# A four-layer trunk on one core: input combinations traced in five pieces, MLP loads held back, other buffers for the gating layer's first weights

## The chip, the core and the metric

The kernel runs on one core of a Trainium2 chip. The engines it uses are TensorE (PE: matmuls, and PEld for the weight loads that overlap them), VectorE (DVE), ScalarE (ACT), GpSimd (POOL: a few small operations and the DMAs that add into their target) and SyncE (SP: the plain loads). The metric is the device time of one execution in microseconds, as the median of several.

## What is computed

A trunk of two token mixers, each followed by a dense MLP, for one sequence of 512 tokens and a width of 1024, all in float32:

```python
def sq_relu_mlp(h, w_up, w_down):
    return jnp.square(jax.nn.relu(h @ w_up)) @ w_down

def chunked_sgu_mixer(h, w_in, ln_g, ln_b, w_spatial, b_spatial, w_out):
    z = jax.nn.gelu(h @ w_in, approximate=False)
    u, v = jnp.split(z, 2, axis=-1)
    v = layer_norm(v, ln_g, ln_b)
    # 128x128 lower triangular mixing of positions, one matrix per channel group
    v = ...
    return (u * v) @ w_out

# layer 0: latent attention, MLP; layer 1: spatial gating, MLP; every one is
# x = x + f(rms_norm(x)); a last rms_norm at the end
```

The gating layer's `w_in` is 1024 x 4096 and its `w_out` 2048 x 1024; each MLP's `w_up` is 1024 x 4096 and `w_down` 4096 x 1024.

## The kernel before

The stages run one after the other: attention until about 170 us of the trace, the first MLP until about 503, the gating layer until about 770, the second MLP until 1098. PE does the products of the last three as sums of three fp32r products: each operand is split into a high part, a cast on ACT (`split`, L125; `wh` for a weight, `g` or `q` for an activation), and a low part, a subtraction on DVE (`low`, L122; `wl` for a weight), and high x high, high x low and low x high are added in PSUM (L110).

On top of this, the large products use a scheme of seven block products instead of eight for 2 x 2 blocks. The blocks of the normed input are A11, A12, A21, A22, and the seven left operands are A11, A12, A22, S3 = A11 - A21, N1 = A22 - A21, S2 = -N1 - A11 and S4 = -A12 - S2. `Quarters` makes them: `first` makes A11 and S3, `rest` transposes the second half of the input (`turn`: PE transposes, then ACT scales one half of each of four banks into A12 and DVE the other into A22) and makes the five others. Each of the seven is split in a high and a low part. The weights' combinations come from DMAs: a block is loaded by SP (`load`, L991), and others are added into the same buffer by POOL's accumulating DMA (`add`, L994) once the buffer's earlier content has been split.

An *item* is one block product: `prepare` fetches and splits its weights, `go` issues its matmuls (48 of 256 columns in an MLP, 24 of 512 columns in the gating layer) and what uses its sum. Items are traced in a list; each is prepared two items ahead. The program of every engine is then ordered by a scheduler that follows the traced order and its own estimate of when data is there, so code that is traced at another place moves instructions on ACT and DVE. All loads on SP stand in one queue and all accumulations on POOL in another; each waits for its target buffer to be free.

In an MLP (`ffn`, `up`) the first items are m1 (A11, weights b), m5 (S3, weights a), m2 (A12, weights c), m6 (S2, weights a + b), m7 (N1, weights p3: b with a block added), m3 (A22, weights p4: a with a block added), m4 (S4). They are called items 0 to 6 below. Items 0, 3, 4 and 6 add into the same two PSUM banks X; between items 3 and 4 ACT copies both banks out (`keep`, L1073), and item 4 adds on. The raw weights are in six buffers (`raws`), two of them shared with the stage before. All of `rest` was traced right behind item 0.

The gating layer begins with `gate(0)` and `gate(1)`, whose items alternate: A11 of both (items 0 and 1), A12 of both (items 2 and 3), N1 of both, S4 of both, and so on. Items 2 and 3 use weights c and c1. Before, both were loaded into one buffer, W, so the load of c1 waited for the split of c. The other raw buffers are R1, R2, and U1 and U2, the halves of `u0`; `rest` wrote A12, A22 and N1 into `u0` too, so U1 and U2 came free only behind it.

Of the kernel before, what the change touches and what calls it, by code (L numbers as in the profile page):

```python
# [10 lines left out]
F32 = mybir.dt.float32  # L11
# [6 lines left out]
P = 128  # L18
T = 512
# [38 lines left out]
def trunk(ctx: ExitStack, tc: tile.TileContext, a):  # L58
# [10 lines left out]
    def nm(s):  # L69
        count[0] += 1  # L70
        return f"{s}_{count[0]}"
# [21 lines left out]
    def tmp(shape=(P, T), tag="t", **kw):  # L93
        return scratch[-1].tile(list(shape), F32, tag=tag, name=nm(tag), **kw)
# [19 lines left out]
    def gpair(t=None):  # L114
# [3 lines left out]
        t = t.rearrange("p k n -> p (k n)")  # L118
        return t[:, 0:T], t[:, T : 2 * T]

    def low(eng, l, src, h):
        return eng.tensor_sub(l, src, h.bitcast(F32))  # L122

    def split(hl, src, eng=None):
        nc.scalar.copy(hl[0], src)  # L125
        low(eng or nc.vector, hl[1], src, hl[0])
        return hl
# [103 lines left out]
    def diagonals(r):  # L231
        dg = tmp((P, NT, P))
        nc.vector.tensor_tensor(
            out=dg, in0=ident.unsqueeze(1).broadcast_to([P, NT, P]),
            in1=r.unsqueeze(2).broadcast_to([P, NT, P]), op=ALU.mult,
        )
        return dg.rearrange("p i q -> p (i q)")

    def row_form(dg, parts=False):

        ps = psum()
        if not parts:
            nc.tensor.matmul(ps, lhsT=ones, rhs=dg, start=True, stop=True)
        else:
            h, l = dg
            nc.tensor.matmul(ps, lhsT=ones_r, rhs=h, start=True, stop=False)
            nc.tensor.matmul(ps, lhsT=ones_r, rhs=l, start=False, stop=True)
        rb = tmp(tag="rb", bufs=1)
        nc.scalar.copy(rb, ps)
        return rb  # L250

# [38 lines left out]
    def four(dtype=F32R):  # L290
        return gxp.tile([P, 4, H], dtype, tag="g", name=nm("g"))
# [7 lines left out]
    class Quarters:  # L299
# [28 lines left out]

        def rest(self, a12, a22, n1):

            self.turn(1, a12, a22)
            stt = nc.vector.scalar_tensor_tensor
            nc.vector.tensor_sub(n1, a22, self.a21)
            s2, s4 = self.a11, a12
            stt(out=s2, in0=n1, scalar=-1.0, in1=self.a11, op0=ALU.mult, op1=ALU.subtract)
            self.A12 = split((four(), G6[0]), a12)
            stt(out=s4, in0=a12, scalar=-1.0, in1=s2, op0=ALU.mult, op1=ALU.subtract)
            self.S2 = split((G6[1], G6[2]), s2)
            self.N1 = split((G6[3], G6[4]), n1)
            self.A22 = split((G6[5], four()), a22)  # L340
            self.S4 = split((four(), four()), s4)

# [215 lines left out]
    with tc.tile_pool(name="att", bufs=1) as att:  # L560
# [356 lines left out]
        def go(n):  # L917
            for _ in range(min(n, len(waiting))):
                waiting.pop(0)()
# [76 lines left out]
    def ffn(layer, xq, norm, pool, after=None, last=None, mid=None):  # L996
# [24 lines left out]
        def up(c):  # L1021
# [116 lines left out]
            m3 = item(p4, "A22", "Y", False, end3, True)  # L1138
            m4 = item(w22, "S4", "X", False, end4, True)
            if c == 0:  # L1140
                begin = m1[1]

                def first():
                    begin()
                    three = [squares.get() for _ in range(3)]
                    xq.rest(*three)
                    for t in three:
                        squares.put(t)
                    nc.vector.reciprocal(r2, norm.mean())
                    nc.vector.tensor_scalar(  # L1150
                        out=nr2, in0=r2, scalar1=-1.0, scalar2=None, op0=ALU.mult
                    )

                return [(m1[0], first), m5, m2, m6, m7, m3, m4], sq
            return [m1, m2, m5, m6, m7, m3, m4], sq

        def accumulate(i, u, ps, r):
# [131 lines left out]
        n_mixed = len(work)  # L1289
        if last is None:  # L1290
            work += down(3, sq)
        ahead = 2
        for prepare, _ in work[:ahead]:
            prepare()
        for j, (_, go) in enumerate(work):
            if j == 1:
                spare[:] = banks[6:8]
            if j == 7:
                spare[:] = []
            if j == n_mixed:  # L1300
                spare[:] = banks[0:2]
            go()
            if j + ahead < len(work):
                work[j + ahead][0]()
        if last is not None:
            spare[:] = banks
            last(
# [23 lines left out]
    gx2 = Quarters("norm_ffn", KD, 1)  # L1331
    with stage(1), tc.tile_pool(name="sgu", bufs=1) as sg:
        w_in, w_out = a["sgu_w_in"][0], a["sgu_w_out"][0]
        wt = sg.tile([P, 8, P], F32, name="wt")
        Bt = sg.tile([P, 16, P], F32, name="Bt")


        v = [sg.tile([P, NT, 1024], F32, name=nm("v")) for _ in range(2)]
        stats = sg.tile([P, P], F32, name="stats")
        st = stats[:, 0:96].rearrange("p (i c e) -> p i c e", i=NT, c=4)  # L1340
        mv = stats[:, 96:104].rearrange("p (i e) -> p i e", e=2)

        names = ("a11", "a12", "a21", "a22")
        u0 = sg.tile([P, NT, 1024], F32, name="u0")
        uq = [
            {t: o[:, n, :].rearrange("p (k n) -> p k n", k=4) for n, t in enumerate(names)}
            for o in (u0, v[0])
# [7 lines left out]


        R1, R2 = (raw_tile((P, 4, 512)) for _ in range(2))
        W = sg.tile([P, 4, 512], F32, name=nm("wb"))
        U1, U2 = halves_of(u0)
        V1, V2 = halves_of(v[1])  # L1360
        BT = Bt.rearrange("p (k a) t -> p k (a t)", k=4)
# [105 lines left out]
        def gate(c, X, Y, slots):  # L1467
            sa, sb, sc = slots
            na, nb = f"a{c}", f"b{c}"

            def w(k, u):
                return wview(w_in, gx1.row(k), 512, SGW + c * 1024 + u * 512, 512)

            def at(name, b):

                t, u = int(name[1]) - 1, int(name[2]) - 1
                i = 2 * t + b
                return i, v[c][:, i, u * 512 : (u + 1) * 512], st[:, i, 2 * c + u, :]

            def keep(name, acc):  # L1480
                for b in range(2):
                    nc.scalar.copy(at(name, b)[1], acc[b])

            def plus(name, acc):
                for b in range(2):
                    t = at(name, b)[1]
                    nc.vector.tensor_add(t, t, acc[b])

            def gelu(name, r, acc=None):
                for b in range(2):  # L1490
                    i, t, sums = at(name, b)
                    nc.scalar.activation(
                        t, t if acc is None else acc[b], AF.Gelu, scale=norms[r][:, i : i + 1]
                    )
                    nc.vector.bn_stats(out=sums, in_=t)

            def end1():
                keep("a11", X)

            def end2():  # L1500
                plus("a11", Y)
                gelu("a11", "r")

            def end5():
                keep("a22", Y)

            def end3():
                keep("a12", Y)

            def end6():  # L1510
                plus("a12", X)
                gelu("a12", "nr")

            def end7():
                plus("a22", X)
                gelu("a22", "nr")

            def end4():
                gelu("a21", "r", X)

            def p2():
                nc.vector.tensor_add(s[na], s[na], s[nb])

            def item(acc, first, left, *args):
                return rows_item(acc, first, lambda: getattr(gx1, left), *args)

            return [
                item(X, True, "A11", na, lambda: get(na, sa, w(0, 0)), end1),
                item(Y, True, "A12", "c", lambda: get("c", sc, w(1, 0)), end2),
                item(Y, True, "N1", na, lambda: add(sa, w(0, 1)), end5),  # L1530
                item(Y, False, "S4", nb, lambda: get(nb, sb, w(1, 1)), end3, p2),
                item(X, False, "S2", na, lambda: None, end6),
                item(X, False, "S3", nb, lambda: add(sb, w(0, 1)), end7),
                item(X, False, "A22", na, lambda: add(sa, w(1, 0)), end4),
            ]
# [101 lines left out]
        def outer(X, Y, Z):  # L1637
# [64 lines left out]
            return items  # L1702

        work = [
            i for two in zip(gate(0, A, E, (R1, U1, W)), gate(1, B, C, (R2, U2, W))) for i in two
        ]
        work += other(0, A, E, C, (R1, W, R2, W)) + other(1, C, E, A, (R2, R1, W, R1))
        work += outer(A, C, E)
# [2 lines left out]
        def after(n, f):  # L1711
            then.setdefault(n, []).append(f)

        def begin():
            gx1.rest(*(uq[0][t] for t in ("a11", "a12", "a21")))
            r = inv_sqrt(norm1.mean())
            with tc.issue_after(root[0].ins):
                mix_load()
            norms["r"], norms["nr"] = r, small()
            nc.vector.tensor_scalar(  # L1720
                out=norms["nr"], in0=r, scalar1=-1.0, scalar2=None, op0=ALU.mult
            )

        def rows_of_r():
            norms["rb"] = row_form(diagonals(norms["r"]))

        def deviations():
            for i in range(NT):
# [20 lines left out]
            spare[:] = t  # L1749

        after(0, begin)
        after(6, lambda: banks_are(E))
        after(8, rows_of_r)
        after(9, lambda: (mix_transposed(0), mix_transposed(1)))
# [20 lines left out]
        ahead = 2  # L1775
        for prepare, _ in work[:ahead]:
            prepare()
        for j, (_, go) in enumerate(work):
            go()
            for f in then.get(j, ()):  # L1780
                f()
            if j + ahead < len(work):
                work[j + ahead][0]()
        fixed[0] = None


# [115 lines left out]
```

## Time and profile before

| | |
|---|---|
| median of 3 runs | 1096.78 us (1094.18 to 1101.85) |
| the profiled execution | 1099.8 us, of which its span is 1098.1 us |
| busy share of the span | PE 97%, PEld 87%, DVE 79%, ACT 57%, POOL 12% |
| mean granted clock of PE | 0.984 of full speed |
| moved by DMA | 163.33 MB, 149 GB/s in the mean |
| share of the chain that ended last | PE 84%, DVE 7%, DMA 3%, ACT 3% |

The profile is of one execution. A row of the timeline gives the start and the busy time of an instruction or a run of like ones, and in brackets how long its engine stood still before it and which instruction released it. The windows give each engine's busy time in a stretch and PE's granted clock there. PE is the engine that is hardly ever idle, so its few idle times and its stretches at a lower clock are what to look for; idle time of ACT or DVE matters only where PE waits for what they do next.

### The profile page before, as it was taken

Reading aid. Unit: us, or ns where it says so; the run is one execution under the profiler, and the core shown is the slowest. Engines: PE = TensorE matmul, PEld = TensorE weight load, DVE = VectorE, ACT = ScalarE, POOL = GpSimd, SP = SyncE. Lnnn points to the kernel's source line nnn. Section 1 sums busy time; section 2 is a strip of 40 time slices with the busy share of each in tenths; the row PEclk is TensorE's granted clock in tenths of the full one; section 3 lists DMA queues with packets and bytes.
Section 4 is the critical chain, followed back from the end, with each engine's and each line's share of the span. In section 5 each row is a group of like instructions: output and inputs, shape, how many; then the busy total and the mean of one; then the engine's idle time right before and its main releaser. Section 6 shows DMA issues by size and latency. Waiting matters only on the chain.

```text
span 1098.1 us, 15748 instructions
## 1 busy us (share of the span) xinstructions
PE 1062.3 (97%) x6540; PEld 950.8 (87%) x6540; DVE 865.7 (79%) x947; ACT 628.7 (57%) x714; POOL 128.3 (12%) x155
## 2 busy tenths in 40 slices
PE   8799999999999999999899999999999999999997
PEld 6688888999998999877788999888899999999986
DVE  6988756897887887886868588997988788888753
ACT  4577646665655655646655635556775555556541
POOL 5510000001001001003011000110001001001000
PEclk9999999899999999989899999999999999999999
DMA  6120147668668759348386836876785876756431
GB/s 203 39 78 16 63 115 220 181 147 176 197 153 192 178 135 224 116 77 192 116 158 140 236 71 201 230 121 166 173 228 120 221 196 115 224 125 117 116 113 58
DMA packets 86083, 163.33 MB, mean 149 GB/s; under 512 B 4917, under 2 KB 10620, under 8 KB 85884
## 3 DMA queue, kind: packets, MB, share of 16 engines
q0 software_dynamic: 33584, 67.11, 35.1%
q1 hardware_dynamic: 52428, 95.22, 25.3%
q8 instruction: 51, 0.84, 0.3%
q14 instruction: 20, 0.16, 0.0%
HBM read 160.22 MB, written 2.10 MB: 148 GB/s over the span
## 4 chain that ended last, share of the span: by engine, by line
PE 84%; DVE 7%; DMA 3%; ACT 3%; issue 2%; POOL 0%; SPq 0%; POOLq 0%; ACTq 0%; DVEq 0%
PE ps L110 79%; DVE wl L122 2%; DMA wb<-in_sgu_w_in 2%; ACT wh L125 2%; PE ps L1617 1%; DVE g L122 1%; PE ps L856 1%; DMA wb<-in_ffn_w_up 1%; DVE sq L485 1%; PE ps L296 1%; ACT p L836 0%; ACT v L1743 0%; PE ps L826 0%; PE ps L824 0%; PE ps L823 0%
## 5 line engine op out<-in xcount | busy, mean ns | idle before, releaser
L110 PE MATMUL ps<-g,wh 128*128 128x256 f32 (+1 forms) x2304 | 422.6, 286 | 9.4 <-DVE g L122 4.9
L110 PEld LDWEIGHTS ps<-g,wh 128*128 128x128 f32 x2304 | 361.3, 191 | 17.3 <-DVE g L122 5.7
L110 PE MATMUL ps<-g,wl 128*128 128x256 f32 (+1 forms) x1152 | 328.1, 285 | 0.6 <-DVE wl L122 0.6
L110 PE MATMUL ps<-wh,q 128*128 128x512 f32 (+1 forms) x840 | 267.3, 391 | 2.7 <-DVE x L1159 2.7
L122 DVE TENSOR_TENSOR wl<-wb,wh 128x2048 fp32r<-128x2048 f32 x75 | 171.7, 2289 | 69.8 <-ACT wh L125 69.8
L110 PEld LDWEIGHTS ps<-g,wl 128*128 128x128 f32 x1152 | 218.9, 190 | 2.2 <-DVE wl L122 0.9
L125 ACT CAST wh<-wb 128x2048 fp32r<-128x2048 f32 x75 | 143.1, 1907 | 120.4 <-PE ps L110 91.6
L110 PEld LDWEIGHTS ps<-wh,q 128*128 128x128 f32 x840 | 158.7, 189 | 34.9 <-issue 3.1
L122 DVE TENSOR_TENSOR wl<-wr,wh 128x2048 fp32r<-128x2048 f32 (+1 forms) x69 | 153.3, 2225 | 38.0 <-ACT wh L125 38.0
L125 ACT CAST wh<-wr 128x2048 fp32r<-128x2048 f32 (+1 forms) x69 | 127.8, 1855 | 69.9 <-PE ps L110 49.9
L110 PE MATMUL ps<-wl,q 128*128 128x512 f32 (+1 forms) x420 | 164.3, 391 | 0.0
L110 PE MATMUL ps<-wh,g 128*128 128x512 f32 x496 | 158.2, 397 | 2.1 <-DVE g L122 1.3
L110 PEld LDWEIGHTS ps<-wh,g 128*128 128x128 f32 x496 | 94.2, 190 | 23.6 <-DVE g L122 1.7
L125 ACT CAST q<-sq 128x1024 fp32r<-128x1024 f32 x51 | 53.6, 1051 | 90.1 <-PE ps L110 87.5
L110 PE MATMUL ps<-wl,g 128*128 128x512 f32 x248 | 98.1, 396 | 3.4 <-DVE wl L122 3.4
L110 PEld LDWEIGHTS ps<-wl,q 128*128 128x128 f32 x420 | 79.8, 190 | 14.8
L1159 DVE SCALAR_TENSOR_TENSOR x<-ps,s,x 128x512 f32<-128x512 f32 x98 | 72.6, 746 | 22.3 <-PE ps L110 22.3
L122 DVE TENSOR_TENSOR q<-sq,q 128x1024 fp32r<-128x1024 f32 x51 | 62.3, 1222 | 4.9 <-ACT q L125 1.8
L110 PEld LDWEIGHTS ps<-wl,g 128*128 128x128 f32 x248 | 47.4, 191 | 14.2 <-DVE wl L122 4.1
L994 POOL DMA_DIRECT2D wr<-in_ffn_w_up x16 | 20.9, 1307 | 270.7 <-DMA wr<-in_ffn_w_up 107.0
L994 POOL DMA_DIRECT2D wb<-in_ffn_w_down x17 | 21.9, 1291 | 133.6 <-DVE wl L122 131.7
L1076 DVE TENSOR_TENSOR sq<-sq,ps 128x512 f32<-128x512 f32 x48 | 32.6, 681 | 4.4 <-PE ps L110 3.0
(269 smaller groups left out, 1289.2 us busy)
## 6 DMA issues: line engine op xcount, KB each, us to landing
wb<-in_ffn_w_up SPq DMA_DIRECT2D x18, 1024.0 KB, 5.7
wb<-in_ffn_w_down SPq DMA_DIRECT2D x18, 1024.0 KB, 5.1
wb<-in_ffn_w_down POOLq DMA_DIRECT2D x17, 1024.0 KB, 8.7
wr<-in_ffn_w_up POOLq DMA_DIRECT2D x16, 1024.0 KB, 8.6
wr<-in_ffn_w_up SPq DMA_DIRECT2D x14, 1024.0 KB, 5.6
wr<-in_sgu_w_in POOLq DMA_DIRECT2D x9, 1024.0 KB, 11.0
wr<-in_ffn_w_down SPq DMA_DIRECT2D x8, 1024.0 KB, 5.5
wb<-in_ffn_w_up POOLq DMA_DIRECT2D x8, 1024.0 KB, 8.7
```

The costliest lines, as they stand in the source:

```text
L110: nc.tensor.matmul(out, lhsT=lhsT, rhs=rhs, start=start and t == 0, stop=stop and t == 2, **kw)
L122: return eng.tensor_sub(l, src, h.bitcast(F32))
L125: nc.scalar.copy(hl[0], src)
L296: nc.tensor.transpose(ps[:, i * P : (i + 1) * P], x[:, i, k * P : (k + 1) * P], ident)
L485: nc.vector.tensor_tensor_reduce(out=junk, in0=x[:, i, cuts[c] * P : cuts[c + 1] * P], in1=x[:, i, cuts[c] * P : cuts[c + 1] * P], scale=1 ...
L856: nc.tensor.transpose(ps[b][:, c : c + P], pr[h, i][:, j * P : (j + 1) * P], ident)
L994: nc.gpsimd.dma_start(t, src, accum_op=ALU.add)
L1076: both(name, lambda t, j: nc.vector.tensor_add(t, t, pv(acc[sums][j])))
L1159: nc.vector.scalar_tensor_tensor(out=xs, in0=ps, scalar=r[:, i : i + 1], in1=xs, op0=ALU.mult, op1=ALU.add)
L1617: nc.tensor.matmul(ps[:, i * P : (i + 1) * P], lhsT=m[:, i, :], rhs=wt[:, j // 2, :], start=True, stop=True,)
```

## The change

It has three parts. `rest` becomes five closures that are traced at different items: `second` (the turn and A12), `differences` (N1), `sums` (S2), `others` (A22) and `last` (S4). In the MLPs `second` follows item 0, `differences` and `sums` item 1, `others` and `last` item 3; in the gating layer they follow items 0 to 4. In the MLPs, after item 0 and the preparing of item 2, one element of every free raw buffer is set to zero by DVE, at the earliest behind the low part of item 2's weights (`issue_after`), so that the loads into these buffers wait for it. In the gating layer the pools' order changes, c1 is loaded into U1 and S4's first weights into U2, `rest` writes into `Bt` and `wt` instead of `u0`, and the row of r has its own tile.

```diff
+    newest = [None]
+
     def low(eng, l, src, h):
-        return eng.tensor_sub(l, src, h.bitcast(F32))
+        newest[0] = eng.tensor_sub(l, src, h.bitcast(F32))
+        return newest[0]
...
         def rest(self, a12, a22, n1):
 
-            self.turn(1, a12, a22)
             stt = nc.vector.scalar_tensor_tensor
-            nc.vector.tensor_sub(n1, a22, self.a21)
             s2, s4 = self.a11, a12
-            stt(out=s2, in0=n1, scalar=-1.0, in1=self.a11, op0=ALU.mult, op1=ALU.subtract)
-            self.A12 = split((four(), G6[0]), a12)
-            stt(out=s4, in0=a12, scalar=-1.0, in1=s2, op0=ALU.mult, op1=ALU.subtract)
-            self.S2 = split((G6[1], G6[2]), s2)
-            self.N1 = split((G6[3], G6[4]), n1)
-            self.A22 = split((G6[5], four()), a22)
-            self.S4 = split((four(), four()), s4)
+
+            def second():
+                self.turn(1, a12, a22)
+                self.A12 = split((four(), G6[0]), a12)
+
+            def differences():
+                nc.vector.tensor_sub(n1, a22, self.a21)
+                self.N1 = split((G6[3], G6[4]), n1)
+
+            def sums():
+                stt(out=s2, in0=n1, scalar=-1.0, in1=self.a11, op0=ALU.mult, op1=ALU.subtract)
+                self.S2 = split((G6[1], G6[2]), s2)
+
+            def others():
+                self.A22 = split((G6[5], four()), a22)
+
+            def last():
+                stt(out=s4, in0=a12, scalar=-1.0, in1=s2, op0=ALU.mult, op1=ALU.subtract)
+                self.S4 = split((four(), four()), s4)
+
+            return second, differences, sums, others, last
...
+        three = [squares.get() for _ in range(3)]
+        second, differences, sums, others, final = xq.rest(*three)
...
+        then = {
+            0: [second], 1: [differences, sums, scales], 3: [others, final],
+            4: [lambda: [squares.put(t) for t in three]],
+        }
         ahead = 2
+
+        def run(lo, hi):
+            for j in range(lo, hi):
...
+                work[j][1]()
+                for f in then.get(j, ()):
+                    f()
+                if j + ahead < len(work):
+                    work[j + ahead][0]()
+                if j == 0:
+
+                    with tc.issue_after(newest[0].ins):
+                        for t in raws.free:
+                            nc.vector.memset(t[:, 0, 0:1], 0.0)
...
-            i for two in zip(gate(0, A, E, (R1, U1, W)), gate(1, B, C, (R2, U2, W))) for i in two
+            i for two in zip(gate(0, A, E, (R1, U2, W)), gate(1, B, C, (R2, W, U1))) for i in two
...
+        wide = Bt.rearrange("p (e k a) t -> p e k (a t)", e=2, k=4)
+        rest = gx1.rest(wide[:, 0], wide[:, 1], wt.rearrange("p (k a) t -> p k (a t)", k=4))
+
         def begin():
-            gx1.rest(*(uq[0][t] for t in ("a11", "a12", "a21")))
+            rest[0]()
...
         after(0, begin)
+        after(1, rest[1])
+        after(2, rest[2])
+        after(3, rest[4])
+        after(4, rest[3])
```

Three places of the engines' programs, as they stand in a row. First DVE at the first MLP's start, before, from the last turn on. The first row is the turn, the second wl of weights a, then n1, A12's low (`g_0`), s2, N1's low (`g_4`), s4, S2's low (`g_2`):

```order
L317 TENSOR_SCALAR sq_2049<-ps_2061,G 128x256
L122 TENSOR_TENSOR wl_2234<-wr_2042,wh_2233 128x2048
L333 TENSOR_TENSOR sq_2050<-sq_2049,g_1953 128x1024
L122 TENSOR_TENSOR g_0_2026<-sq_2048,g_2149 128x1024
L335 SCALAR_TENSOR_TENSOR g_1952<-sq_2050,g_1952 128x1024
L122 TENSOR_TENSOR g_4_2030<-sq_2050,g_3_2029 128x1024
L337 SCALAR_TENSOR_TENSOR sq_2048<-sq_2048,g_1952 128x1024
L122 TENSOR_TENSOR g_2_2028<-g_1952,g_1_2027 128x1024
```

The same place of the change:

```order
L320 TENSOR_SCALAR sq_2048<-ps_2061,G 128x256
L1324 MEMSET wb_2044 128x1
L1324 MEMSET wb_2045 128x1
L1324 MEMSET wb_2046 128x1
L1324 MEMSET wb_2043 128x1
L342 TENSOR_TENSOR sq_2049<-sq_2048,g_1953 128x1024
L124 TENSOR_TENSOR g_0_2026<-sq_2047,g_2147 128x1024
L346 SCALAR_TENSOR_TENSOR g_1952<-sq_2049,g_1952 128x1024
L124 TENSOR_TENSOR g_4_2030<-sq_2049,g_3_2029 128x1024
L124 TENSOR_TENSOR wl_2230<-wr_2042,wh_2229 128x2048
L124 TENSOR_TENSOR g_2_2028<-g_1952,g_1_2027 128x1024
```

The wl of weights a has moved behind N1's low, and the memsets stand where it was.

Second ACT in the same MLP, some items later, before. `wh_2345` is the cast of p4, the two copies are those of the banks X behind item 3, `wh_2402` is item 6's weights:

```order
L125 CAST wh_2345<-wr_2042 128x2048
L1080 ACTIVATE sq_2047<-sq_2047 128x1024
L1073 COPY sq_2052<-ps_2054 128x512
L1081 ACTIVATE sq_2047<-sq_2047 128x1024
L125 CAST q_2515<-sq_2047 128x1024
L1073 COPY sq_2052<-ps_2055 128x512
L125 CAST wh_2402<-wb_2044 128x2048
```

And with the change:

```order
L1095 ACTIVATE sq_2050<-sq_2050 128x1024
L1096 ACTIVATE sq_2050<-sq_2050 128x1024
L1088 COPY sq_2052<-ps_2054 128x512
L128 CAST q_2519<-sq_2050 128x1024
L128 CAST wh_2349<-wr_2042 128x2048
L1088 COPY sq_2052<-ps_2055 128x512
L128 CAST g_2344<-sq_2047 128x1024
L128 CAST wh_2406<-wb_2044 128x2048
```

The cast of p4 now stands between the two copies, directly ahead of the second bank's.

Third DVE at the gating layer's start, before: wl of c (`wl_4855`), the four turns, A12's low (`g_0`), and, further down than these rows go, wl of c1:

```order
L122 TENSOR_TENSOR wl_4855<-wb_4746,wh_4854 128x2048
L317 TENSOR_SCALAR u_4743<-ps_4753,G 128x256
L317 TENSOR_SCALAR u_4743<-ps_4754,G 128x256
L317 TENSOR_SCALAR u_4743<-ps_4751,G 128x256
L317 TENSOR_SCALAR u_4743<-ps_4752,G 128x256
L122 TENSOR_TENSOR g_0_2026<-u_4743,g_4817 128x1024
```

With the change the first turn stands well ahead, and from wl of c (`wl_4846`) on it reads:

```order
L124 TENSOR_TENSOR wl_4846<-wb_4743,wh_4845 128x2048
L320 TENSOR_SCALAR Bt<-ps_4759,G 128x256
L320 TENSOR_SCALAR Bt<-ps_4756,G 128x256
L124 TENSOR_TENSOR wl_4880<-u_4744,wh_4879 128x2048
L320 TENSOR_SCALAR Bt<-ps_4757,G 128x256
L124 TENSOR_TENSOR g_0_2026<-Bt,g_4820 128x1024
```

The wl of c1 (`wl_4880`) stands ahead of the last turn and of A12's low. ACT has the same order: the cast of c1 (`wh_4879`) stands ahead of its last turn and of A12's cast (`g_4820`):

```order
L128 CAST wh_4845<-wb_4743 128x2048
L1508 COPY v_4742<-ps_4755 128x512
L319 ACTIVATE Bt<-ps_4759,G 128x256
L319 ACTIVATE Bt<-ps_4756,G 128x256
L128 CAST wh_4879<-u_4744 128x2048
L319 ACTIVATE Bt<-ps_4757,G 128x256
L128 CAST g_4820<-Bt 128x1024
```

Before, those casts stood the other way round: A12's was the next after the four turns, c1's came four casts and copies later.

## Rows read from the trace of the kernel before

**Rows 1.** PE waits of the whole span: us in total, times, longest.

```profile
PE ps L110 <- DVE g L122: 6.1, 4, 3.2
PE ps L110 <- DVE wl L122: 4.1, 2, 3.4
...
PE ps L110 <- DVE x L1159: 2.7, 1, 2.7
```

**Rows 2.** Timeline of PE, first MLP: start, busy us, form, idle before, releaser.

```profile
190.39 0.50 PE L110 MATMUL ps<-g,wh 128*128 128x256 f32 x2 [0.98 <-ACT g L125]
194.07 0.58 PE L110 MATMUL ps<-g,wh 128*128 128x256 f32 x1 [3.17 <-DVE g L122]
```

**Rows 3.** Timeline of PE at the gating layer's start.

```profile
517.05 0.50 PE L110 MATMUL ps<-wh,g 128*128 128x512 f32 x1 [0.71 <-ACT g L125]
...
519.05 0.73 PE L110 MATMUL ps<-wh,g 128*128 128x512 f32 x2 [1.26 <-DVE g L122]
...
523.94 0.84 PE L110 MATMUL ps<-wh,g 128*128 128x512 f32 x3
528.22 0.80 PE L110 MATMUL ps<-wl,g 128*128 128x512 f32 x1 [3.44 <-DVE wl L122]
```

**Rows 4.** Windows: busy us per engine (instructions), then clock, DMA share, GB/s.

```profile
176.00:189.40 13.40, 13.40 (x114) 13.16 (x112) 6.29 (x12) 8.23 (x14) 0.00 (x0) 1.00 1.06 347
194.00:199.50 5.50, 5.43 (x25) 5.43 (x26) 5.50 (x6) 3.10 (x4) 0.00 (x0) 0.50 1.08 180
487.00:493.50 6.50, 6.24 (x15) 4.92 (x16) 6.24 (x5) 4.33 (x7) 0.00 (x0) 0.51 0.01 3
528.20:534.30 6.10, 6.08 (x14) 4.81 (x15) 6.10 (x7) 3.67 (x4) 0.00 (x0) 0.50 0.81 275
```

**Rows 5.** Timeline of ACT in the first MLP.

```profile
183.75 1.90 ACT L125 CAST wh<-wb 128x2048 fp32r<-128x2048 f32 x1 [3.94 <-DMA wb<-in_ffn_w_up]
...
202.19 1.91 ACT L125 CAST wh<-wr 128x2048 fp32r<-128x2048 f32 x1 [3.69 <-PE ps L110]
...
207.74 0.59 ACT L1073 COPY sq<-ps 128x512 f32<-128x512 f32 x1
...
213.07 1.91 ACT L125 CAST wh<-wb 128x2048 fp32r<-128x2048 f32 x1 [2.93 <-PE ps L110]
```

**Rows 6.** Timeline of DVE in the first MLP: wl of a, A12's low.

```profile
189.46 2.28 DVE L122 TENSOR_TENSOR wl<-wr,wh 128x2048 fp32r<-128x2048 f32 x1
...
192.80 1.22 DVE L122 TENSOR_TENSOR g<-sq,g 128x1024 fp32r<-128x1024 f32 x1
```

**Rows 7.** Timeline of SP's queue: loads at both stages' starts (start, us from first to last).

```profile
176.42 1.78 SPq L991 DMA_DIRECT2D wb<-in_ffn_w_up  x3
...
503.34 13.36 SPq L991 DMA_DIRECT2D wb<-in_sgu_w_in  x2
```

**Rows 8.** Timeline of POOL: two accumulating DMAs of the first MLP.

```profile
171.37 1.30 POOL L994 DMA_DIRECT2D wr<-in_ffn_w_up  x1 [18.16 <-ACT g L316]
192.04 1.28 POOL L994 DMA_DIRECT2D wr<-in_ffn_w_up  x1 [19.38 <-DVE wl L122]
```

**Rows 9.** DMA view, stretches from 191.5, 500, 516: KB each, median us to landing.

```profile
wr<-in_ffn_w_up POOLq DMA_DIRECT2D x1, 1024.0 KB, 8.4
...
wr<-in_sgu_w_in POOLq DMA_DIRECT2D x1, 1024.0 KB, 9.8
wb<-in_sgu_w_in SPq DMA_DIRECT2D x1, 1024.0 KB, 8.7
v<-in_sgu_w_spatial POOLq DMA_DIRECT2D x2, 256.0 KB, 3.9
...
wb<-in_sgu_w_in SPq DMA_DIRECT2D x1, 1024.0 KB, 5.5
```

**Rows 10.** Timeline of ACT at the gating layer's start: A12's cast.

```profile
515.96 1.05 ACT L125 CAST g<-u 128x1024 fp32r<-128x1024 f32 x1
```

**Rows 11.** Timeline of PE at the second MLP's start.

```profile
791.96 0.38 PE L110 MATMUL ps<-g,wh 128*128 128x256 f32 x1 [0.89 <-DVE g L122]
```

More of the change, by code (lines that the diff above doesn't have):

```diff
@@ L237, in diagonals, with row_form @@
         return dg.rearrange("p i q -> p (i q)")
-    def row_form(dg, parts=False):
+    def row_form(dg, parts=False, rb=None):
         ps = psum()
@@ L247, in row_form @@
             nc.tensor.matmul(ps, lhsT=ones_r, rhs=l, start=False, stop=True)
-        rb = tmp(tag="rb", bufs=1)
+        rb = rb or tmp(tag="rb", bufs=1)
         nc.scalar.copy(rb, ps)
@@ L1140, in up @@
             if c == 0:
[L1141 to L1154, printed above, removed]
+                return [m1, m5, m2, m6, m7, m3, m4], sq
             return [m1, m2, m5, m6, m7, m3, m4], sq
@@ L1291, in ffn, with scales @@
             work += down(3, sq)
-        ahead = 2
+        three = [squares.get() for _ in range(3)]
+        second, differences, sums, others, final = xq.rest(*three)
+        def scales():
+            nc.vector.reciprocal(r2, norm.mean())
+            nc.vector.tensor_scalar(out=nr2, in0=r2, scalar1=-1.0, scalar2=None, op0=ALU.mult)
+        then = {
+            0: [second], 1: [differences, sums, scales], 3: [others, final],
+            4: [lambda: [squares.put(t) for t in three]],
+        }
+        ahead = 2
+        def run(lo, hi):
+            for j in range(lo, hi):
+                if j == 1:
+                    spare[:] = banks[6:8]
+                if j == 7:
+                    spare[:] = []
+                if j == n_mixed:
+                    spare[:] = banks[0:2]
+                work[j][1]()
[7 more added lines that the diff above has]
+                            nc.vector.memset(t[:, 0, 0:1], 0.0)
         for prepare, _ in work[:ahead]:
             prepare()
[L1295 to L1304, printed above, removed]
+        run(0, len(work))
         if last is not None:
@@ L1333, in trunk @@
         w_in, w_out = a["sgu_w_in"][0], a["sgu_w_out"][0]
+        v = [sg.tile([P, NT, 1024], F32, name=nm("v"))]
+        W = sg.tile([P, 4, 512], F32, name=nm("wb"))
+        u0 = sg.tile([P, NT, 1024], F32, name="u0")
+        v.append(sg.tile([P, NT, 1024], F32, name=nm("v")))
         wt = sg.tile([P, 8, P], F32, name="wt")
         Bt = sg.tile([P, 16, P], F32, name="Bt")
-        v = [sg.tile([P, NT, 1024], F32, name=nm("v")) for _ in range(2)]
+        rb_row = sg.tile([P, T], F32, name="rb")
         stats = sg.tile([P, P], F32, name="stats")
@@ L1343, in trunk @@
         names = ("a11", "a12", "a21", "a22")
-        u0 = sg.tile([P, NT, 1024], F32, name="u0")
         uq = [
@@ L1357, in trunk @@
         R1, R2 = (raw_tile((P, 4, 512)) for _ in range(2))
-        W = sg.tile([P, 4, 512], F32, name=nm("wb"))
         U1, U2 = halves_of(u0)
@@ L1724, in rows_of_r @@
         def rows_of_r():
-            norms["rb"] = row_form(diagonals(norms["r"]))
+            norms["rb"] = row_form(diagonals(norms["r"]), rb=rb_row)
         def deviations():
@@ L1777, in trunk, with run @@
             prepare()
[L1778 to L1783, printed above, removed]
+        def run(lo, hi):
+            for j in range(lo, hi):
+                work[j][1]()
+                for f in then.get(j, ()):
+                    f()
+                if j + ahead < len(work):
+                    work[j + ahead][0]()
+        run(0, len(work))
         fixed[0] = None
```

## The prediction

> **What bounds the kernel now.** By the page TensorE (PE) is busy 97% of the span, so the change can win only where PE stands still or runs at the lower clock. I therefore read the PE waits first, sorted by what ended them: the two largest groups are `low` subtractions of DVE (L122), 6.1 us in four waits and 4.1 in two [rows 1]. The timeline says where: at the first MLP's start 0.98 and 3.17 [rows 2], at the gating layer's start 0.71, 1.26 and 3.44 [rows 3]. Then the windows, for the clock: behind the two long waits the granted clock is 0.50 (1.2 GHz instead of 2.4) for 5.5 and 6.1 us, which costs half of each, 2.75 and 3.05 us [rows 4]. So the first MLP's start loses 0.98 + 3.17 + 2.75 = 6.9 us, the gating layer's 0.71 + 1.26 + 3.44 + 3.05 = 8.5. At the second MLP's start only a wait of 0.89 is worth naming [rows 11]. That is some 16 us to be won at most.
>
> **First MLP, DVE's order.** DVE is released by the cast of the c weights (ACT, 183.75 to 185.65), which waited 3.94 us for their load [rows 5]. Then DVE does wl of c, four turns until 189.5, wl of a (2.28), n1 until 192.8, and the subtraction for A12 that PE waits for, ending 194.0 [rows 2, 6]. After the change wl of a stands behind A12, N1's low and s2; in its place are four memsets. No memset of this shape is in the trace: at the least they cost nothing, at the most each what the shortest group here, the subtraction for A12, takes for 1024 elements, 1.22, so 4.9 for four; with one element each they are nearer nothing, and I take 0.1 each, 0.4. A12's low now ends at 194.0 - 2.2 + 0.4 = 192.2, less what the load gains.
>
> That gain is the hold-back's. Now c is issued at 176.42 with other loads right behind it and lands 7.3 us later, beside an accumulation issued at 171.37 [rows 5, 7, 8]. Alone, 1 MB takes 5.5; beside accumulations another took 8.7 [rows 9]. The gain lies between 0 and 1.8; I take 0.2, since the accumulation stays beside it and 7.3 is already under 8.7. The Trainium skill, "DMA: Bandwidth & Descriptors", section "Queues, rings and completion order", says that each DMA engine consumes one queue row's descriptors in ring order and goes round robin between rows, so loads queued behind c take nothing from it: by that rule the gain is 0, by the lone row 1.8.
>
> So PE waits about 0.8 and 1.4 instead of 0.98 and 3.17, and the third matmul of item 2 runs at 192.0 instead of 194.07. Whether the clock then falls is open: it stayed up after 0.71 + 1.26 [rows 3] and fell after 2.73 [rows 1, 4]. The sum, 2.2, lies between: even odds.
>
> **What is late next there.** wl of a ends at about 196.4 instead of 191.7, and the accumulation of p4 into the same buffer waits for it: it was issued at 192.04 and took 8.4 [rows 8, 9]; now it goes at 196.7. The held-back loads (one into each of four buffers, 4 MB, released at 190) lie beside it. Bounds: 8.4 alone, 9.8 as for the accumulation beside which W is loaded [rows 9], and, if all that is left of the loads (2.7 MB at 347 GB/s [rows 4], 7.8 us) goes first, 16. I take 9.6: landing at 206.3. Before, ACT cast p4 at 202.19, after its landing, and copied the second bank of item 3's sum at 207.74 [rows 5]. Now that cast stands ahead of this copy: 206.3 + 1.9 + 0.6 = 208.8. An item takes (213.07 - 202.19) / 2 = 5.44 us [rows 5], so item 2 ends at 192.0 + 5.2 = 197.2, item 3 (whose S2 low ends at 197.6, 0.3 late) at 203.0, and the second half of item 4, which adds onto the copied bank, is due at 205.7: **a new wait of 3.1 us**. Item 5 starts at 208.8 + 2.7 = 211.5 instead of 212.9: a gain of 1.4 if the clock stays up at both places. If it falls at the first, item 4 is due 2.75 later, the new wait shrinks to 0.4, and the end is 211.5 again. If it stays up at the first and falls at the second, 2.75 goes: -1.3. Weighed, **+0.8**.
>
> **Gating layer.** c of the second half (c1) no longer waits for W. Before, W was issued at 503.34 and landed 8.7 later, at 512.0 [rows 7, 9]; c1 was issued when wl of W was done, at 516.3, took 5.5, and PE got its wl at 528.2 [rows 3, 9]. After, c1 goes out right behind W, and a third load behind it. One transfer later (1 MB at 347 GB/s, 3.0 us) is 515.1; but four loads of 256 KB of the mixing weights, some 4 us each, are issued by POOL near 510 [rows 9], so I take 516.0, with 515.1 and 517.5 as ends. That removes the 3.44.
>
> But ACT now casts c1 ahead of the fourth turn of A12, and DVE does wl of c1 ahead of its last turn and of A12's low. ACT: cast of W until 514.0, a copy and two turns until 515.2, then it stands until c1 lands; cast 516.0 to 517.9, last turn 518.3, cast for A12 519.3 (before: 517.0 [rows 10]). DVE: wl of c1 517.9 to 520.2, turn 520.6, A12's low 521.8 (before 519.0). Item 1 ends at 516.3. So **PE waits 3.0 and 2.0 at item 2**, where it waited 0.71 and 1.26, then runs items 2 and 3 through. From 521.8 there are 46 matmuls of (523.94 - 519.05) / 21 = 0.23 [rows 3], 10.6: item 4 at 532.4 at full clock. Before: from 528.22, 14 matmuls at half speed until 534.3 [rows 4] and 8 more, 1.9: 536.2. A wait of 3.0 is longer than the 2.73 after which the clock fell, so I let it fall: 3.05 back, item 4 at 535.4, **+0.8**; with c1 at 515.1 it is 1.7, at 517.5 it is -0.7. With the clock up, 3.8.
>
> **Second MLP.** The wait of 0.89 is for S2's low [rows 11], which stood behind s4, as long as A12's low, 1.22 [rows 6]; now it stands behind one `plus` of half the size, 0.6: -0.6. The held loads move beside the accumulations there, whose casts have several us until they are due, and the memsets stand ahead of a wl that waits for ACT anyway. I count **+0.4**.
>
> **Rest.** The row of r in a tile of its own and the pools' new order move nothing that PE waits for: 0. Sum: 0.8 + 0.8 + 0.4 = 2.0 us. The profiled execution took 1099.8 (span 1098.1) and would take 1097.8; the median of the runs, 1096.8, is 3 lower, and becomes **1094.8**.
>
> **Rivals.**
> (a) *The gating layer's clock stays up.* For it: after 0.71 + 1.26 it did. Against it: one wait is 3.0 now. It gives 3.8 there, with c1 at 515.1 4.7; with p4 landing after 8.4 the first MLP gives 2.6. In all 6 to 8 us: 1089 to 1091.
> (b) *Slower: p4 is starved by the loads released into it.* After 13 us it lands at 209.7, the copy ends at 212.2, the new wait is 6.5 and drops the clock: item 5 at 212.2 + 2.7 + 2.75 = 217.7, 4.8 later than now; the sum becomes 0.8 + 0.4 - 4.8 = -3.6: 1100.4. It turns to a loss there from a landing at 205.0 with a fallen clock, at 207.7 without. For it: 8.4 became 9.8 with one load beside it [rows 9]. Against it: it takes 16 us only if all loads go first.
> (c) *What is won is waited for elsewhere:* the hold-back gives c nothing, item 4 of the first MLP and item 2 of the gating layer take the rest: 1096 to 1098. The ring rule named above is its first half.
>
> **Numbers.** Forecast 0.45 (1092 to 1096), (a) 0.22, (b) 0.13, (c) 0.2. The range for 8 in 10 goes from 1088 to 1099.5. A change under 1%, 11 us, can hardly be told from none here (the three runs before span 7.7). Faster by 11 needs both clocks up, an early c1 and nothing new to wait for: 0.07. Slower by 11 needs (b) in both MLPs and a late c1: 0.03. Between: 0.9.
>
> **What would show it.** Right: p4 issued near 196.5, a PE wait of 2 to 4 us near 206 that ACT's copy (L1088) ends; in the gating layer c1 landing near 516, a PE wait of 2 to 3.5 ended by ACT's g near 519, another by DVE's g near 522, and none for wl at item 3. Wrong: no PE wait at item 4 (the first MLP then gives 4 or more), c's load under 6 us (the hold-back works), a granted clock of 1.00 from 516 to 530, or c1 landing after 518.

## The result and the profile after

The changed kernel takes 1106.72 us (1105.56 to 1108.35, 4 runs) beside 1095.48 us before (1091.49 to 1101.85, 4 runs): the ratio is 1.0103, with a 95% interval from 1.0079 to 1.0126. It is slower by 8.6 to 13.8 us, where 2.0 less was forecast.

The profiled execution took 1105.56 us, its span is 1103.9. Its PE waits, read as in [rows 1] (us in total, times, longest), are led by a group that was not there before:

```profile
PE ps L110 <- ACT sq L1088: 11.4, 2, 7.6
PE ps L110 <- ACT g L128: 6.6, 4, 4.2
PE ps L110 <- DVE g L124: 3.6, 4, 1.2
```

L1088 is the copy of a bank X between items 3 and 4 of an MLP. The two waits of DVE's L122 (now L124) that the change was to shorten fell from 6.1 + 4.1 us to 3.6 + 0.6; in their place stand 11.4 us for that copy. The timeline of PE says where, at item 4 of the first MLP, at item 2 of the gating layer, at item 4 of the second MLP:

```profile
191.64 0.38 PE L110 MATMUL ps<-g,wh 128*128 128x256 f32 x1 [1.10 <-DVE g L124]
213.19 0.79 PE L110 MATMUL ps<-g,wh 128*128 128x256 f32 x2 [7.63 <-ACT sq L1088]
...
524.89 0.80 PE L110 MATMUL ps<-wh,g 128*128 128x512 f32 x1 [4.16 <-ACT g L128]
527.29 1.22 PE L110 MATMUL ps<-wh,g 128*128 128x512 f32 x2 [1.18 <-DVE g L124]
...
800.86 0.80 PE L110 MATMUL ps<-g,wh 128*128 128x256 f32 x2 [3.73 <-ACT sq L1088]
```

The first row answers to [rows 2]: the wait of 3.17 for A12's low has become 1.10. The third and fourth answer to [rows 3]: 0.71, 1.26 and 3.44 have become 4.16 and 1.18, with no wait at item 3. The second and the last are new. Behind them the clock falls, as the windows show (columns as in [rows 4]):

```profile
213.00:217.50 4.50, 4.31 (x22) 4.31 (x23) 4.50 (x4) 2.89 (x3) 0.00 (x0) 0.55 0.29 64
801.00:804.00 3.00, 3.00 (x14) 3.00 (x15) 1.27 (x2) 3.00 (x3) 0.00 (x0) 0.50 0.67 195
```

ACT, POOL and the DMA view say what the copy waited for. First ACT in the first MLP, in place of [rows 5], and its cast of p4 in the second; then POOL's accumulation of p4, in place of the second of [rows 8]; then its time to landing in the first and in the second MLP, in place of the first of [rows 9]:

```profile
200.95 1.05 ACT L128 CAST q<-sq 128x1024 fp32r<-128x1024 f32 x1
210.76 1.90 ACT L128 CAST wh<-wr 128x2048 fp32r<-128x2048 f32 x1 [8.76 <-DMA wr<-in_ffn_w_up]
212.56 0.58 ACT L1088 COPY sq<-ps 128x512 f32<-128x512 f32 x1
...
796.38 1.90 ACT L128 CAST wh<-wr 128x2048 fp32r<-128x2048 f32 x1 [6.78 <-DMA wr<-in_ffn_w_up]
```

```profile
196.61 1.28 POOL L1009 DMA_DIRECT2D wr<-in_ffn_w_up  x1 [23.76 <-DVE wl L124]
```

```profile
wr<-in_ffn_w_up POOLq DMA_DIRECT2D x1, 1024.0 KB, 14.1
```

```profile
wr<-in_ffn_w_up POOLq DMA_DIRECT2D x1, 1024.0 KB, 13.5
```

p4 is issued at 196.61 and lands 14.1 us later. ACT stands in front of its cast for 8.76 us, and the copy that PE needs is the next instruction. The profile before has 8.4 and 8.6 us for these two accumulations.

To sum up by stage, four places of PE in both traces. Before:

```profile
487.26 0.76 PE L110 MATMUL ps<-wh,q 128*128 128x512 f32 x1 [2.73 <-DVE x L1159]
...
503.33 0.50 PE L110 MATMUL ps<-wh,g 128*128 128x512 f32 x1
...
625.20 0.50 PE L110 MATMUL ps<-g,wh 128*128 128x256 f32 x2 [1.81 <-ACT u L1550]
...
770.92 0.50 PE L110 MATMUL ps<-g,wh 128*128 128x256 f32 x2 [1.02 <-ACT g L125]
```

After:

```profile
492.05 0.47 PE L110 MATMUL ps<-wh,q 128*128 128x512 f32 x1 [2.68 <-DVE x L1161]
...
507.72 0.50 PE L110 MATMUL ps<-wh,g 128*128 128x512 f32 x1 [0.95 <-ACT g L128]
...
628.50 0.51 PE L110 MATMUL ps<-g,wh 128*128 128x256 f32 x2 [1.73 <-ACT u L1576]
...
770.92 0.51 PE L110 MATMUL ps<-g,wh 128*128 128x256 f32 x2 [1.02 <-ACT g L128]
```

The first MLP lost 492.05 - 487.26 = 4.8 us (0.2 of it lie before the MLP), the stretch to the gating layer's middle won 4.8 - 3.3 = 1.5, the stretch to 771 won 3.3, and the second MLP lost all of 1103.9 - 1098.1 = 5.8.

Neither win is the change's. The 1.5 are the clock behind the wait at the end of the first MLP, which is 2.73 us long before and 2.68 after: from 487 to 493.5 the granted clock is 0.51 before [rows 4], and at the same place after it is higher (the last but two column):

```profile
492.00:498.50 6.50, 6.45 (x21) 5.18 (x22) 6.03 (x4) 4.43 (x7) 0.00 (x0) 0.74 0.01 3
```

That is 6.5 us at 0.23 more. What the gating layer's part itself changed is about nothing: from item 0 to the middle it won 1.1 (121.9 us before, 120.8 after), and ahead of item 0 there is a new wait of 0.95.

The 3.3 stand in code that is the same in both kernels. Over the traces below, this stretch takes 142.4 to 145.7 us, and a kernel with the old gating layer (the second of the two on the MLPs' order) takes 763.53 - 621.10 = 142.4 like the change. Behind the wait of 1.81 at 625.20 the clock fell in the trace before, and behind 1.73 at 628.50 it did not in the trace after (the granted clock of 622 to 630; after, it is 1.00 from 628.5 to 636.5 as well):

```profile
622.00:630.00 8.00, 6.19 (x40) 5.99 (x40) 4.97 (x5) 2.91 (x3) 0.00 (x0) 0.79 0.40 133
```

```profile
622.00:630.00 8.00, 6.27 (x55) 6.07 (x54) 2.75 (x2) 3.28 (x4) 0.00 (x0) 1.00 0.60 222
```

That is 8 us at 0.21 less, 1.7 of the 3.3; the rest I did not trace. So the two profiled executions differ by 5.8 us and the timed medians by 11.2; without the 3.3 and the 1.5 the traces differ by 10.6, inside the interval.

### The profile page after: what moved, and what is told of

It is laid out like the page before. It is cut to its first block, busy times and chain, and to the rows that moved or that the text cites. A ratio compares the mean times of both kernels' runs of the same rounds, so it can differ in the third digit from the quotient of the medians.

```text
span 1103.9 us, 15753 instructions
## 1 busy us (share of the span) xinstructions
PE 1058.8 (96%) x6540; PEld 947.7 (86%) x6540; DVE 865.5 (78%) x955; ACT 627.7 (57%) x714; POOL 128.8 (12%) x155
## 4 chain that ended last, share of the span: by engine, by line
PE 77%; DMA 7%; DVE 7%; issue 4%; ACT 4%; POOL 0%; SPq 0%; POOLq 0%; ACTq 0%; DVEq 0%
PE ps L110 72%; DMA wr<-in_ffn_w_up 3%; DVE wl L124 2%; ACT wh L128 2%; DMA wb<-in_ffn_w_down 1%; DMA u<-in_sgu_w_in 1%; PE ps L1643 1%; DMA wb<-in_sgu_w_in 1%; PE ps L871 1%; DMA wb<-in_ffn_w_up 1%; DVE sq L500 1%; PE ps L299 1%; ACT p L851 0%; DVE g L124 0%; PE ps L841 0%
## 5 line engine op out<-in xcount | busy, mean ns | idle before, releaser
L110 PE MATMUL ps<-g,wh 128*128 128x256 f32 (+1 forms) x2304 | 421.4, 285 | 17.7 <-ACT sq L1088 11.4
L124 DVE TENSOR_TENSOR wl<-wb,wh 128x2048 fp32r<-128x2048 f32 x76 | 173.9, 2289 | 67.6 <-ACT wh L128 67.5
L124 DVE TENSOR_TENSOR wl<-wr,wh 128x2048 fp32r<-128x2048 f32 (+1 forms) x69 | 153.4, 2225 | 47.7 <-ACT wh L128 47.7
L124 DVE TENSOR_TENSOR q<-sq,q 128x1024 fp32r<-128x1024 f32 x51 | 62.3, 1222 | 5.1 <-ACT q L128 2.0
```

The costliest lines, as they stand in the source:

```text
L110: nc.tensor.matmul(out, lhsT=lhsT, rhs=rhs, start=start and t == 0, stop=stop and t == 2, **kw)
L124: newest[0] = eng.tensor_sub(l, src, h.bitcast(F32))
```

## The experiments

All times are beside runs of the kernel before on the same chip. Traces of different runs begin up to 3 us apart, so durations and waits are compared, not places.

**Which part costs: four kernels.** Theory A: the held-back loads starve the accumulation of p4. Theory B: the order costs, since p4's cast stands on ACT ahead of something that PE needs earlier. The first leaves the four memsets out:

```diff
-                if j == 0:
-                    with tc.issue_after(newest[0].ins):
-                        for t in raws.free:
-                            nc.vector.memset(t[:, 0, 0:1], 0.0)
```

> The change without the four memsets: rest in five pieces and the gating layer's buffers stay, no load of the MLPs is held back. Theory A (the held-back loads starve the accumulation of p4, which took 14.1 us in the first MLP and 13.5 in the second instead of 8.4 and 8.6): p4 lands within 10 us of its issue in both MLPs, the PE waits of 7.6 and 3.7 us ended by ACT's copy of the second bank are gone, and the time is 7 to 11 us below that of the change, about 1096 to 1100. Theory B (what costs is the order: the cast of p4 stands on ACT ahead of something that PE needs earlier, whatever the loads do): in this kernel the cast of p4 stands ahead of the cast of S2's high part, so with p4 landing near 200.5 PE waits some 5 us at item 3 of the first MLP, for S2, and the time is within 4 us of the change, 1103 to 1108.

Measured: 1101.96 us, ratio 1.006 [1.004, 1.0081]. p4 took 8.6 and 8.5 us, and of the two waits for the copy 0.4 us is left. But the gain over the change is about 5, not 7 to 11, and the time lies between the two forecasts, since in the first MLP PE waited elsewhere:

```profile
195.16 0.39 PE L110 MATMUL ps<-g,wh 128*128 128x256 f32 x1 [2.04 <-DVE g L124]
204.91 0.74 PE L110 MATMUL ps<-g,wh 128*128 128x256 f32 x4 [2.54 <-ACT wh L128]
```

Without the held loads the scheduler's order puts p4's cast even ahead of the cast of S2's high part, and item 3 waits (2.5 us and two shorter ones). Both theories hold a part: A for the length of p4, and for all of the second MLP, from item 0 to the end 327.2 us as before (1098.1 - 770.92, and 1100.2 - 773.03); B for the first.

The second adds only the hold-back to the kernel before.

> The kernel before with only the hold-back of the MLP loads added. Theory A: p4 takes 12 to 15 us in both MLPs since the held loads lie beside it, PE waits 5 to 9 us at item 4 or 5 of the first MLP and 3 to 5 us in the second, and the time is 8 to 14 us above the kernel before. Theory B: the same late cast with p4 taking 8.4 to 10 us, 2 to 6 us above the kernel before. If c's load gains from the hold-back, it lands in 5.5 to 6 us instead of 7.3.

Measured: 1109.73 us, 1.0125 [1.0095, 1.0155], the time that A says. p4 took 13.7 us in the second MLP and 10.6 in the first, less than the 12 forecast; there it was issued later still, at 203.85. Its PE waits:

```profile
PE ps L110 <- ACT sq L1076: 8.8, 2, 4.5
PE ps L110 <- DVE wl L124: 6.8, 3, 3.3
```

The first row is the copy again, 4.27 and 4.53. The second holds a new wait of 2.91 us in the first MLP: with the memsets in its list the scheduler put wl of weights a (their buffer holds the a + b of item 3 by then) behind eight subtractions and sums of `rest`. It began at 201.02, at 189.46 before, so here the hold-back cost by the order as well as by p4's delay:

```profile
203.36 0.58 PE L110 MATMUL ps<-g,wl 128*128 128x256 f32 x1 [2.91 <-DVE wl L124]
```

Alone, the hold-back costs no less than the whole change; the intervals overlap. And c gained nothing: from issue to ACT's cast it took 7.2 us here, 6.8 in the change, 7.3 before; over the other kernels 6.4 to 7.0 with the four loads held, 6.4 to 7.5 without, and 8.5 in the kernel below that holds two.

The third is the gating layer's part alone, the fourth the MLPs' parts alone.

> The gating layer's part alone (its buffers, and its rest in five pieces), the MLPs as before. In the changed kernel's trace this part gave back 1.5 us up to item 4, so both theories say 0.5 to 3 us below the kernel before, about 1093 to 1095, with a PE wait of 3.5 to 4.5 us at item 2 that ACT's cast for A12 ends. A rival: c1 lands late only because the two accumulations before it came late too, after the first MLP's delay; then c1 lands near 516, the wait is under 3.2 and the gain 3 us or more.

> The change without the gating layer's part: rest in five pieces and the hold-back in the MLPs alone. Both theories: all that was lost is in the MLPs, so this is 1 to 3 us above the change, 1107 to 1111, with the same PE waits of 7 to 8 and 3.5 to 4 us ended by ACT's copy. If it comes out below the change, the gating layer's part costs time.

Measured: 1096.2 us, 1.0008 [0.9988, 1.0029], and 1104.89 us, 1.0082 [1.005, 1.0114]. The gating part is worth nothing that can be measured; its wait for A12's cast is there with the old MLPs too (4.33 us), so c1's lateness does not come from the first MLP's delay. The wait of 0.95 at item 0 comes with this part too: it is in all ten traces that have it and in none of the four others. The MLP part alone loses nearly all, with waits for the copy of 7.25 and 3.99. It came out a little below the change (1104.9, where 1107 to 1111 was expected), so the gating layer's part gave the change nothing here; the intervals overlap.

**Gating layer: place in the order, or the load?** The gating part alone, and one edge more: c1's cast and low part behind A12's (`cast[0]` is the newest cast; `behind` puts what is traced under it behind the given instructions).

```diff
+        a12 = []
         def begin():
             rest[0]()
+            a12[:] = cast[0], newest[0]
...
-                if j + ahead < len(work):
+                if j + ahead == 3:
+                    with behind(a12):
+                        work[3][0]()
+                elif j + ahead < len(work):
                     work[j + ahead][0]()
```

> The gating layer's part alone, MLPs as before, with one edge more: the cast and the low part of c1 are put behind the cast and the low part of A12 on ACT and DVE. Theory O (the gating layer's new wait at item 2 comes from the place of c1's split in the order): A12's cast no longer waits for c1, PE waits under 1 and about 1.2 us at item 2 and not at item 3, the clock stays up, and the time is 5 to 8 us below the gating part alone, 1088 to 1091. Rival L (the load of c1 itself comes too late for item 3, whatever the order): a wait of 2 us or more at item 3 ended by wl, and a time within 3 us of the gating part alone.

Measured: 1090.65 us, 0.9951 [0.9936, 0.9967], inside the range of theory O. Without the edge, and then with it, PE at items 2 and 3:

```profile
522.15 0.79 PE L110 MATMUL ps<-wh,g 128*128 128x512 f32 x1 [4.33 <-ACT g L128]
524.56 1.22 PE L110 MATMUL ps<-wh,g 128*128 128x512 f32 x2 [1.18 <-DVE g L124]
```

```profile
519.54 0.73 PE L110 MATMUL ps<-wh,g 128*128 128x512 f32 x2 [1.49 <-DVE g L124]
```

With the edge the gating part, whose point is the early load of c1, is worth some 5 us; the place of c1's cast in the order took it all.

**The MLPs: place in the order, or p4's landing?** The first of two kernels keeps the hold-back and puts p4's cast behind the copy (an `issue_after` on ACT); the second drops the hold-back and has the same edge and one more, weights a's low behind A12's on DVE, so that ACT and DVE have the same order in the first MLP in both. The line of m6 is in the second kernel alone; its `a12[0]` is A12's low part.

```diff
                 def prepare():
                     name = weights()
-                    ww.extend(split(wtiles(4, 512, 16), s[name]))
+                    with ExitStack() as es:
+                        if edge is not None and c == 0:
+                            es.enter_context(tc.issue_after(edge().ins))
+                        ww.extend(split(wtiles(4, 512, 16), s[name]))
...
-            m6 = item(p2, "S2", "X", False, end6)
+            m6 = item(p2, "S2", "X", False, end6, False, lambda: a12[0])
...
-            m3 = item(p4, "A22", "Y", False, end3, True)
+            m3 = item(p4, "A22", "Y", False, end3, True, lambda: copies[-1])
```

> The changed kernel with one edge more: in the MLPs the cast of p4 is put behind the copy of the second bank on ACT. Theory A (p4 itself lands too late, 14 us after a late issue): the wait at item 4 of the first MLP goes, but item 5 then waits for p4, some 6 us from 208.6 to 214.9, so the first MLP gains 2 us at most; in the second MLP p4 lands in time for item 5 and its 3.7 us and the clock come back, about 5.5 us; 1098 to 1101. Theory B (only the place of the cast costs): no wait at item 5 and all that was lost comes back, 1092 to 1095.

> The MLPs' rest in five pieces without the hold-back, the gating layer as before, with two edges: the low part of weights a behind the low part of A12 on DVE, and the cast of p4 behind the copy of the second bank on ACT. This gives the same order on ACT and DVE there as the kernel with the late cast and the hold-back, so the two differ by the held-back loads alone. Theory A (the loads starve p4): p4 takes 8.4 to 10 us instead of 14, PE waits under 1 us at item 5 and about 0.8 and 1.2 at item 2; 3 to 6 us below the kernel before, 1089 to 1092, and 6 to 9 below the kernel with the hold-back. Theory B: within 2 us of the kernel with the late cast and the hold-back.

Measured: 1099.24 us, 1.0036 [1.0018, 1.0053], and 1092.78 us, 0.9976 [0.9959, 0.9992]. With the hold-back p4 took 12.7 and 13.6 us, and in the first MLP PE waited for it at item 5 instead:

```profile
213.97 0.51 PE L110 MATMUL ps<-g,wh 128*128 128x256 f32 x2 [1.69 <-ACT wh L128]
216.29 0.58 PE L110 MATMUL ps<-g,wl 128*128 128x256 f32 x1 [1.82 <-DVE wl L124]
```

In the second MLP, where p4 is due later, no wait is left. So the place of the cast decides what p4's delay costs, and the held loads make the delay: without them p4 takes 8.5 and 8.4 us. The two kernels differ by 6.5 us, where theory A said 6 to 9 and B under 2. They differ in the gating layer's part too, but that was worth nothing measurable. The second kernel waits 0.9 us in its second MLP, where the new edge on DVE itself issues p4 later.

**How much held load makes how much delay.** The late cast again, holding only the first two of the four buffers (`raws.free[:2]`).

> The changed kernel with the late cast of p4, holding back only the loads into the first two of the four free buffers; same order on ACT and DVE. Theory A in its simplest form (p4 shares the engines with what is left of the held loads): about half of the delay, p4 takes 10 to 12 us instead of 12.7 to 14.1 (8.5 without a held load), in both MLPs, and the time is 1 to 4 us below the late cast with four. If p4 still takes over 12.5, what delays it is not the amount of the held loads.

Measured: 1095.49 us, 0.9984 [0.9966, 1.0002]. p4 took 8.5 us in the first MLP and this in the second:

```profile
wr<-in_ffn_w_up POOLq DMA_DIRECT2D x1, 1024.0 KB, 11.4
```

The second MLP fits "half of the delay" (8.5, 11.4, 13.6 for none, two and four held). The first does not. The trace says why: p4 came 7.4 us behind the first held load in both kernels, but there the last load was issued at 193.05 and landed after 9.0, only 2.1 us behind p4's issue at 199.99; in the change the last was issued at 190.82 and landed after 13.7, 7.9 us behind p4's issue at 196.61. I read this as: what counts is what is still on its way at p4's issue. No run changed that alone. By the ratios this kernel lies 5.7 us below the one with four held, more than the 1 to 4 expected, although c landed later in it (8.5 us) and PE waited 2.1 us for A12's cast in the first MLP.

**Why c1 landed 6 us behind W.** Two kernels, each of one run, on the gating part alone. One was to move the loads of the mixing weights behind item 3; the other holds the load into U2, which is queued behind c1, by a memset behind c1's low part.

> The gating layer's part alone with the four 256 KB loads of the mixing weights moved behind item 3. c1 landed 14 us after its issue, 6 us after W. Theory M (the mixing loads on POOL's queue share the engines with c1): c1 lands 3 to 4 us after W, and PE's wait at item 2 for the cast of A12 falls from 4.3 to under 2. Rival U (the load of U2 queued behind c1 takes its share): c1 still lands 5.5 us or more behind W.

> The gating layer's part alone with the load into U2 held until c1's low part is done, so that no load is queued behind c1 on SP. Theory U: c1 lands 2.5 to 4 us after W instead of 6. Theory M, and the ring order that the notes state: nothing changes, c1 lands 5 to 6 us after W and PE waits 4 us or more at item 2.

Measured: 1098.91 and 1096.83 us; with one run each they are read by their traces. The first did the opposite of what was meant: taken out of `issue_after`, the mixing loads went out with W, at 502.4, and not later. It tells the two apart all the same. ACT's casts of W and of c1, first with the mixing loads early, then with U2 held:

```profile
514.38 1.91 ACT L128 CAST wh<-wb 128x2048 fp32r<-128x2048 f32 x1 [6.82 <-DMA wb<-in_sgu_w_in]
...
517.40 1.90 ACT L128 CAST wh<-u 128x2048 fp32r<-128x2048 f32 x1
```

```profile
511.90 1.91 ACT L128 CAST wh<-wb 128x2048 fp32r<-128x2048 f32 x1 [3.55 <-DMA wb<-in_sgu_w_in]
...
517.69 1.90 ACT L128 CAST wh<-u 128x2048 fp32r<-128x2048 f32 x1 [2.67 <-DMA u<-in_sgu_w_in]
```

With the mixing loads beside W, W landed 12.3 us after its issue instead of 8.7 to 9.0, and c1's cast could start by 3.0 us behind W's. With U2 held, c1 came 5.8 us behind W, no sooner. So the load behind c1 on the same queue takes nothing from it that shows, and the mixing loads on the other queue delay the load that they lie beside: W by 3.3 to 3.6 us in the first kernel, and, I take it, c1 in the change. From its issue to ACT's cast c1 took 14.3 to 14.9 us in all of these; no run kept the mixing loads from both.

**A version that beats both.** All of the change but the hold-back, with the edges of the gating layer and of the MLPs; then the same with the MLP edges in the first MLP alone (`and layer == 0`).

> Rest in five pieces everywhere, the gating layer's new buffers, no hold-back, and the three edges of the two kernels with an ordered gating layer and ordered MLPs. If their gains add, 8 to 13 us below the kernel before, 1082 to 1087.

> The kernel with both parts ordered, with the two MLP edges in the first MLP alone. In the second MLP the edge put weights a behind A12 and p4's accumulation 7 us later than without it, and PE waited 1.8 us for p4 (0.9 in the kernel with the MLPs alone). Without it there the second MLP's order is that of the kernel without hold-back, where it lost nothing against before: 1 to 3 us below the kernel with both parts ordered, 1086 to 1088.5, and no PE wait over 1 us in the second MLP.

Measured: 1089.35 us, 0.9936 [0.9914, 0.9958], and 1087.39 us, 0.9928 [0.9906, 0.9951]. The first missed its range: PE waited 1.83 us for p4 in the second MLP, where the DVE edge delays it. Without that edge the median lies at 1087.4, inside its range, 9 us below the kernel before (8 by the ratio) and 19 below the changed one; the difference between the two is within their intervals.

## Why the prediction was wrong

- **The step that failed** is "I take 9.6" for p4 beside the held-back loads. It took 14.1. The bounds of the text, 8.4 to 16, held it; the value was set by the one accumulation with one load beside it (9.8), while here several were queued: the last of them was on its way for another 7.9 us, about what the text had reckoned for its upper bound (7.8). The issue at 196.7 (measured 196.61), the cast ahead of the copy and a new wait at item 4 were right: the wait was 7.63 instead of 3.1, and the clock fell. The first MLP became 4.8 us slower instead of 0.8 faster.
- **The second MLP** failed by the same term, and there the text did not work it out: "casts have several us until they are due" was held against a p4 of its old length. p4 took 13.5 instead of 8.6, its cast began at 796.38 instead of 791.44, and two ACT operations and the copy that PE needs stood behind it: 3.73 us and a stretch at half speed, 5.8 in all instead of a gain of 0.4. The order rows for this place were not read with a late p4 in mind.
- **The rivals.** Rival (b) had the mechanism and, for the first MLP, the size (4.8 us), with a chance of 0.13; that it would act in both MLPs was given 0.03. It acted in both: 4.8 + 5.8. Rival (c) was right in its first half, that c gains nothing; (a) fell with the clock at the gating layer.
- **c's load.** Gain 0.2 forecast, between 0 and 1.8. Held or not, it took 6.4 to 7.5 us, and 8.5 once, with two loads held. The ring order of the Trainium skill, "DMA: Bandwidth & Descriptors", section "Queues, rings and completion order", gave 0, and the traces agree in that the held loads show no gain beyond this spread. The hold-back won nothing and moved load traffic to where p4 is. That the same section has engines go round robin between queue rows speaks for the delay of p4 and of c1 too; the text used the rule for c alone.
- **First waits of the first MLP.** 0.8 and 1.4 forecast; 1.10 for A12's low and less than 0.5 for its high part measured. The four memsets took 0.08 together, not 0.4. The clock stayed up in the change (1.00 until 206) and fell behind like waits in the late cast kernel (0.7 from 194 to 200): even odds were fair.
- **Gating layer.** W's landing, the place of the two new waits, none at item 3, and a fallen clock were right; the waits were 4.16 and 1.18 instead of 3.0 and 2.0. c1 landed 6.0 us behind W, not 4.0: the mixing loads took more than was allowed for them. "Move nothing that PE waits for: 0" left out the new wait of 0.95 at item 0, whose cause I did not trace. The forecast gain of 0.8 became about nothing in the trace, once the clock's 1.5 is taken off, and -3.2 to +1.3 us in the timed runs of this part alone.

## What to carry to other kernels

Holding loads back did not help the transfer ahead of them on the same queue; it moves the bytes to a later place, and what is in flight there on another queue pays. Before a load is moved, look for the accumulations that will then lie beside it, and at what stands behind their first reader on its engine. And after code is traced in another order, read each place where a cast of late data stands ahead of an instruction that PE needs soon: here one edge at each such place, and no hold-back, turned 11 us lost into 8 or 9 won.

## What was not expected of the hardware

The accumulating DMA of p4, 1 MB, took 8.3 to 8.9 us in the traces without held loads (10.0 once, in the second MLP of the kernel with all edges) and 10.6 to 14.1 with four 1 MB loads released ahead of it. And the clock is no function of the length of a wait alone: behind the wait of the gating layer's middle, 0.84 to 1.96 us in 14 traces, it fell at 1.73, 1.81, 1.87 and 1.93, and stayed up at 1.73, 1.84, 1.95 and 1.96. A term for it belongs in a forecast as odds, not as a threshold.
